# State-space tables for all rows at once on VectorE, each part's injection one part earlier, and half of the modulation rows in the attention-free branch's last product

## The chip, the cores and the metric

The kernel runs on one core of one Trainium2 chip. The metric is the device time of one execution in microseconds (us). Three executions of the kernel before took 1556.84, 1557.27 and 1558.54 us; their median, 1557.27 us, is the time to compare with. The core has five engines with one in-order queue each: PE (TensorE, matmuls), DVE (VectorE), ACT (ScalarE), POOL (GpSimd) and SP, which here only issues DMAs; ACT issues some DMAs too.

## The reference

One decoder block on 1024 rows of width 1024. A conditioning vector gives twelve modulation rows of 512 values (six of 1024). A state-space branch and an attention branch read the same projection; a gated feed-forward follows.

```python
cond = silu(c)
sh1, sc1, g1, sh2, sc2, g2 = split(cond @ w_ada + b_ada, 6)     # 12 pieces of 512 columns, n = 0..11
h = rmsnorm(x, norm1_g) * (1 + sc1) + sh1
u, q, k, v, gate_a, gate_b = split(h @ w_in)
# state-space branch: 32 groups of 16 channels, 64 complex states each
lam_bar = exp(lam * dt);  b_bar = (lam_bar - 1) / lam * b
states  = scan(a * x + bu),  bu = u @ b_bar                       # over the 1024 rows
y = gelu(real(states @ c) + d_skip * u)
y = y * sigmoid(y @ w_glu + b_glu)                                # GLU
y_a = y @ w_a
y_b = stick_breaking_attention(q, k, v) @ w_b
x = x + g1 * ((sigmoid(gate_a) * y_a + sigmoid(gate_b) * y_b) @ w_o)
# modulation by sh2, sc2, then a SwiGLU feed-forward, times g2, and a last rmsnorm
```

## The kernel before

**Stages.** The block runs as a row of stages, and PE works through nearly all of them: the projection to u (0 to 101 us), then a middle stage (101 to 316 us) in which PE makes v (`v_proj`, 16 tiles of 24 matmuls, 128x256) and the first gates (`gate(0, m)`, 16 tiles of 24 matmuls, 128x512) while the state-space branch is worked out in pieces beside it; the GLU (316 to 339); q and k of the first pair of heads (`qk_proj`, 339 to 361); `branch_a`, the product with w_a times the gate (361 to 404); then attention, the output projection and the feed-forward. Each fp32 product is made as three products of split operands (a high part and a low part), and the splits (`wh`, `wl`, `wgh`, `wgl`, line 417 on ACT and line 420 on DVE) are made just ahead of the use of a weight.

**The state-space branch in four parts.** Part m is 8 of the 32 groups. The 1024 rows are cut into 128 chunks of 8: within a chunk the sum is a small dense product, and between chunks a scan over 128 values carries the state. A part has these steps:

- `tables(m)`: POOL makes the rotation tables `tc`, `tn` (128 partitions x 4 x 128) by seven doublings of a complex product (`cmul`, six instructions each, lines 71 to 76), and then the injection `er`, `ei` (two copies, lines 223 and 224, and three doublings). PE transposes the injection (line 236, 8 matmuls), and ACT copies it to `inj`. DVE makes `o` (lines 249 to 251, six instructions of 128x576), PE multiplies it by `bst` (line 259, 16 matmuls), ACT copies that to `rt`, DVE adds the skip (lines 264, 266), and eight DMAs lay it out as `tz`.
- `run(m)`: eight DMAs bring u; PE injects it (line 288, 32 matmuls); DVE turns the result by the tables (lines 296 to 301, six instructions of 128x512) and scans it (line 304, eight instructions). The turn back takes four products: two on DVE (lines 310, 311) and two on POOL (lines 314, 315). DVE combines them into `h` (lines 318 and 319, two instructions each), PE makes y from u and h (lines 326 and 327, 16 matmuls each), ACT copies it, eight DMAs store it to `yD`.

`glu` then loads all of y (`raw`), ACT makes the gelu, and ACT and DVE split it into `yp` (lines 904, 905), which the GLU's matmuls read.

**The modulation rows.** Pieces 0 to 3 of `w_ada` are used at the start. Pieces 4 to 11 go through `ada_rest`: SP loads two of eight slices at a time (`aw`, 512 KB, two buffers), DVE multiplies each slice by its eight values of cond and adds it to `acc` (line 868 first, then seven times line 870), and SP stores `acc` to `aD`. Before, all eight pieces are called in the middle stage, two behind each `run(m)`. The rows are read back after attention.

**What sets the order.** A scheduler at build time gives each engine's queue its order from the program's dependencies and costs; the order in the source is only where it starts. At run time each queue is worked strictly in order and stops where its next instruction's operands are not ready. The pool `scr` has six buffers of 128x576 for temporaries; `acc` has two. `branch_a` has 16 tiles; for each, SP loads a gate tile `sg` (three buffers), ACT takes its sigmoid, PE makes 12 matmuls into `ga` (four PSUM buffers), DVE multiplies (line 951) into `gst`, and ACT's queue stores that to `nD`.

Of the kernel before, what the change touches and what calls it, by code (L numbers as in the profile page):

```python
# [28 lines left out]
class S5:  # L29
# [169 lines left out]
    def tables(self, m):  # L199

        nc, pool, work = self.nc, self.pool, self.work
        v, gp = nc.vector, nc.gpsimd
        r0 = slice(4 * m, 4 * m + 4)
        g0 = slice(8 * m, 8 * m + 8)

        tc_ = work.tile([128, 4, 128], F32, name="tc", bufs=2)
        tn = work.tile([128, 4, 128], F32, name="tn", bufs=2)
        p1 = work.tile([128, 4, 64], F32, name="p1", bufs=1)
        p2 = work.tile([128, 4, 64], F32, name="p2", bufs=1)
        gp.memset(tc_[:, :, 0:1], 1.0)  # L210
        gp.memset(tn[:, :, 0:1], 0.0)
        for k in range(7):
            n = 1 << k
            sh = [128, 4, n]
            self.cmul(gp, tc_[:, :, n:2 * n], tn[:, :, n:2 * n], tc_[:, :, 0:n], tn[:, :, 0:n],
                      self.wr[:, r0, k + 1:k + 2].broadcast_to(sh), self.wi[:, r0, k + 1:k + 2].broadcast_to(sh),
                      p1[:, :, :n], p2[:, :, :n])

        er = self.scr([4, 8, 16])
        ei = self.scr([4, 8, 16])  # L220
        p1 = p1.rearrange("p r (j i) -> p r j i", i=16)
        p2 = p2.rearrange("p r (j i) -> p r j i", i=16)
        gp.tensor_copy(er[:, :, 7], self.bbr[:, r0])
        gp.tensor_copy(ei[:, :, 7], self.bbi[:, r0])
        for n in (1, 2, 4):
            src, dst = slice(8 - n, 8), slice(8 - 2 * n, 8 - n)
            sh = [128, 4, n, 16]
            self.cmul(gp, er[:, :, dst], ei[:, :, dst], er[:, :, src], ei[:, :, src],
                      self.lpr[:, r0, n:n + 1].unsqueeze(3).broadcast_to(sh),
                      self.lpi[:, r0, n:n + 1].unsqueeze(3).broadcast_to(sh),  # L230
                      p1[:, :, :n], p2[:, :, :n])
        inj = work.tile([128, 2, 4, 128], F32, name="inj")
        for k, e in ((0, er), (1, ei)):
# [3 lines left out]
            nc.scalar.copy(inj[:, k].rearrange("p r q -> p (r q)"), ps)  # L237

# [33 lines left out]
        return tc_, tn, inj, o, tz  # L272

    def run(self, m, tabs, u_src, y_dst):
# [3 lines left out]
        tc_, tn, inj, o, tz = tabs  # L278
        u = work.tile([128, 8, 128], F32, name="u")
# [29 lines left out]
        gp = nc.gpsimd.tensor_tensor  # L309
        tt(m1[:, :, a], gr[:, :, a], tc_[:, :, a], ALU.mult)  # L310
        tt(m2[:, :, a], gi[:, :, a], tn[:, :, a], ALU.mult)
        m3 = self.scr([4, 128])
        m4 = self.scr([4, 128])
        gp(m3[:, :, a], gi[:, :, a], tc_[:, :, a], ALU.mult)
        self.last = gp(m4[:, :, a], gr[:, :, a], tn[:, :, a], ALU.mult)
        for g in range(2):
            q = slice(64 * g, 64 * g + 64)
            tt(h[0:64, :, g, b], m1[q, :, a], m2[q, :, a], ALU.subtract)
            tt(h[64:128, :, g, b], m3[q, :, a], m4[q, :, a], ALU.add)
# [71 lines left out]
class Block:  # L391
# [112 lines left out]
    def start(self, const, up, s5p):  # L504
# [5 lines left out]
        self.cond32 = up.tile([P, KT, 32], F32, name="cond32")  # L510
        nc.vector.tensor_scalar(self.cond32, self.cond.unsqueeze(2).broadcast_to([P, KT, 32]), 1.0 / 32.0, None, ALU.mult)
        self.hT = [[self.PA.tile([P, 2, 512], F32R, name="pa") for _ in range(KT)], []]
        with self.pool("s0", 1, side="right") as sp, self.pool("s0a", 1, side="right") as ap, self.pool("s5t", 1, side="right") as st, \
                self.pool("s0p", 1, PSUM) as pp, self.pool("s0t", TPB, PSUM) as tp, self.pool("s0m", 5 - TPB, PSUM) as mp:
            x = [None] * KT
# [31 lines left out]
            def ada(g):  # L547
# [15 lines left out]
                for a in (2 * g, 2 * g + 1):  # L563
                    ws.append(self.u_weight(a, ring=None if a < 3 else (up, "u3h", "u3l", self.wring[0][3], "ws", 2)))
# [292 lines left out]
    def ada_rest(self, n, ap, first):  # L857
# [78 lines left out]
    def branch_a(self, y2p, tp, gp):  # L936
# [352 lines left out]
    def run(self):  # L1289
        tc, nc, i = self.tc, self.nc, self.i  # L1290
        with ExitStack() as es:
# [18 lines left out]
            with ExitStack() as s1:  # L1310
# [6 lines left out]
                with self.pool("us", 1, side="right") as up, self.pool("s5", 1, side="right") as pool:  # L1317
                    self.start(const, up, pool)
                    with self.pool("s5w", 1, side="right") as work, self.pool("vs", 2, side="right") as vp, \
# [3 lines left out]
                        s5.begin(work, psum)  # L1323
                        for m in range(4):
# [7 lines left out]
                with ExitStack() as s3:  # L1332
                    with self.pool("ta", 2, side="right") as tp, \
# [10 lines left out]
                        self.branch_a(y2p, tp, gp)  # L1344
# [73 lines left out]
```

## Time and profile before

| | |
|---|---|
| runs shown | 1556.84, 1557.27, 1558.54 us (median 1557.27) |
| profiled execution | 1554.78 us, of which the span of instructions is 1553.1 us |
| granted TensorE clock, mean | 0.965 |
| PE busy | 1416.7 us (91% of the span) |
| PE weight loads | 1115.9 us (72%) |
| DVE busy | 1060.9 us (68%) |
| ACT busy | 612.8 us (39%) |
| POOL busy | 801.9 us (52%) |
| moved by DMA | 210.46 MB, mean 136 GB/s |

Busy time counts matmuls whose ends are modelled, so 91% on PE is not 91% of PE's peak. In the views below a line "A <- B: t, n" says that engine A stood idle t us in n places until B was done. A window row gives its start and end, its length, then for each engine busy time and, in brackets, the number of instructions that started in it; then the granted clock (1.00 is full), the busy share of the DMA engines (it can pass 1 in a short window) and the GB/s moved. Line numbers are those of the kernel before; in the changed kernel the same statements stand five to nine lines lower.

### The profile page before, as it was taken

What the parts mean: (1) busy time and instruction counts of PE and PEld (TensorE: products, weight loads), DVE (VectorE), ACT (ScalarE), POOL (GpSimd) and SP (SyncE); (2) the same over time, 40 slices, a digit from 0 to 9 for tenths busy, and PEclk for the clock granted to TensorE, in tenths of its full rate; (3) what the DMA queues carried; (4) which work ended last, traced back from release to release, by engine and by line L of the source; (5) the groups of instructions that cost most, each with busy time, mean ns of one, the idle gap of its engine ahead of it and who ended that gap; (6) DMA issues with size and microseconds to landing.
All of it is one profiled execution on the core that took longest, in us unless ns stands there. A gap on an engine that the chain in (4) does not pass through costs nothing.

```text
span 1553.1 us, 18339 instructions
## 1 busy us (share of the span) xinstructions
PE 1416.7 (91%) x6578; PEld 1115.9 (72%) x6578; DVE 1060.9 (68%) x1319; ACT 612.8 (39%) x792; POOL 801.9 (52%) x633
## 2 busy tenths in 40 slices
PE   4898889799999999988799889999999998999995
PEld 2687767678765556556688668888888887788874
DVE  5548777542467676775724797666666767999998
ACT  5431211352466656564314643223332323443323
POOL 2488694010346565642420015555555469698795
PEclk9899899899999999999899999999999999999998
DMA  8456775645424233336343413333333137454412
GB/s 274 171 141 182 180 192 170 178 123 158 144 89 129 82 97 115 109 102 208 118 163 114 138 47 118 108 105 110 107 108 112 63 123 296 149 162 148 122 57 109
DMA packets 180451, 210.46 MB, mean 136 GB/s; under 512 B 28612, under 2 KB 121896, under 8 KB 180360
## 3 DMA queue, kind: packets, MB, share of 16 engines
q1 hardware_dynamic: 169288, 201.29, 41.2%
q10 hardware_dynamic: 11072, 8.00, 1.8%
q8 instruction: 52, 0.85, 0.2%
q14 instruction: 39, 0.32, 0.1%
HBM read 159.18 MB, written 48.89 MB: 134 GB/s over the span
## 4 chain that ended last, share of the span: by engine, by line
PE 30%; DVE 10%; POOL 5%; issue 5%; DMA 1%; ACT 1%; DVEq 0%; POOLq 0%; ACTq 0%
PE tq L1136 12%; PE wo L1136 9%; PE wo L1017 5%; PE gu L1136 3%; POOL pb L1196 1%; POOL pa L1189 1%; DVE f L1220 1%; POOL wb L1218 1%; DMA pa<-in_w_ffn_down_dram 1%; DVE x L1241 1%; DVE pb L1241 1%; POOL x L1196 1%; DVE wl L1216 1%; DVE f L1216 1%; DVE ft L436 1%
## 5 line engine op out<-in xcount | busy, mean ns | idle before, releaser
L436 POOL TENSOR_TENSOR ws<-wb 128x1024 f32<-128x1024 f32 x26 | 64.2, 2471 | 193.4 <-DVE f L1043 90.0
L801 POOL TENSOR_TENSOR wa<-wa,wb 128x1024 f32<-128x1024 f32 (+2 forms) x32 | 81.2, 2538 | 72.8 <-DVE wa L797 49.4
L420 POOL TENSOR_TENSOR wl<-ws,wh 128x1024 fp32r<-128x1024 f32 x14 | 39.0, 2787 | 118.3 <-ACT wh L417 108.1
L769 DVE TENSOR_TENSOR wl<-ws,wh 128x1024 fp32r<-128x1024 f32 (+1 forms) x40 | 52.7, 1317 | 67.4 <-POOL wh L768 67.3
L436 POOL TENSOR_TENSOR wgs<-wb 128x1024 f32<-128x1024 f32 x14 | 35.6, 2542 | 72.7 <-DVE wgl L439 31.2
L802 ACT ACTIVATE wa<-wa 128x1024 f32<-128x1024 f32 (+1 forms) x40 | 38.9, 971 | 82.4 <-POOL wa L801 81.3
L1189 POOL TENSOR_TENSOR pa<-pa,row 128x1024 f32<-128x1024 f32 x22 | 66.1, 3026 | 1.3 <-DMA pa<-in_w_ffn_down_dram 1.3
L870 DVE SCALAR_TENSOR_TENSOR acc<-aw,cond,acc 128x512 f32<-128x512 f32 x56 | 54.2, 970 | 17.6 <-DMA aw<-in_w_ada_dram 17.0
L768 POOL TENSOR_SCALAR wh<-ws 128x1024 fp32r<-128x1024 f32 (+1 forms) x40 | 38.4, 959 | 50.1 <-DVE ws L767 48.8
L1127 POOL TENSOR_TENSOR f<-f,f 128x512 f32<-128x512 f32 x30 | 49.0, 1660 | 26.1 <-DVE f L1117 17.6
L767 DVE SCALAR_TENSOR_TENSOR ws<-wa,ws 128x1024 f32<-128x1024 f32 (+1 forms) x40 | 53.4, 1334 | 13.1 <-ACT ws L766 12.8
L699 PE MATMUL mm<-wa,V 128*64 128x512 f32 (+3 forms) x192 | 40.7, 517 | 20.7 <-ACT wa L802 20.7
L417 ACT CAST wh<-ws 128x1024 fp32r<-128x1024 f32 x28 | 29.2, 1047 | 56.9 <-PE wo L1017 31.6
L764 ACT ACTIVATE ws<-wa 128x1024 f32<-128x1024 f32 (+1 forms) x40 | 38.7, 969 | 29.2 <-DVE wa L761 28.8
L1218 POOL TENSOR_TENSOR wb<-pa 128x512 f32<-128x512 f32 x23 | 40.1, 1753 | 15.7 <-DVE wxl L1216 5.5
L797 DVE TENSOR_TENSOR wa<-wa,acc 128x512 f32<-128x512 f32 (+1 forms) x80 | 46.6, 616 | 1.1 <-PE acc L699 1.1
L1116 ACT ACTIVATE f<-f 128x1024 f32<-128x1024 f32 x22 | 23.3, 1061 | 57.0 <-DVE f L1156 29.5
L699 PE MATMUL z<-q,k 64*128 64x512 f32 (+3 forms) x192 | 41.8, 526 | 2.2 <-DVE gst L951 2.2
L1127 POOL TENSOR_TENSOR f<-f 128x512 f32<-128x512 f32 x20 | 42.2, 2127 | 0.0
L1235 PE MATMUL wo<-f,f 128*128 128x512 f32 x132 | 40.7, 389 | 0.0
L766 ACT ACTIVATE ws<-ws 128x1024 f32<-128x1024 f32 (+1 forms) x40 | 38.9, 974 | 1.1
L765 ACT ACTIVATE ws<-ws 128x1024 f32<-128x1024 f32 (+1 forms) x40 | 38.8, 971 | 1.1
(810 smaller groups left out, 4797.5 us busy)
## 6 DMA issues: line engine op xcount, KB each, us to landing
aw<-in_w_ada_dram SPq DMA_DIRECT2D x32, 512.0 KB
wb<-cD SPq DMA_DIRECT2D x32, 512.0 KB
hD<-f SPq DMA_DIRECT2D x30, 512.0 KB
ws<-in_w_in_dram SPq DMA_DIRECT2D x23, 512.0 KB
wb<-in_w_ffn_gate_dram SPq DMA_DIRECT2D x44, 256.0 KB
wb<-in_w_ffn_up_dram SPq DMA_DIRECT2D x44, 256.0 KB
pa<-in_w_ffn_down_dram SPq DMA_DIRECT2D x22, 512.0 KB
wb<-hD SPq DMA_DIRECT2D x40, 256.0 KB
```

The lines of the kernel that those rows point to most:

```text
L436: (add or nc.gpsimd).tensor_tensor(st, a, b, op)
L699: return self.tc.keep_in_program_order(self.nc.tensor.matmul(*args, **kw))
L767: nc.vector.scalar_tensor_tensor(st, a, 0.0, st, ALU.max, ALU.add)
L769: nc.vector.tensor_tensor(lt, st, ht.bitcast(F32), ALU.subtract)
L797: nc.vector.tensor_tensor(a[:, x, 0:f], a[:, x, 0:f], r[:, x, 0:f], ALU.subtract)
L801: nc.gpsimd.tensor_tensor(a[:, :, o], a[:, :, o], behind[:, :, old], ALU.subtract)
L870: nc.vector.scalar_tensor_tensor(acc, w[:, j], cj, acc, ALU.mult, ALU.add)
L1017: nc.tensor.matmul(ps, lhsT=mg[t // 4][k][:, a, P * (t % 4):P * (t % 4) + P], rhs=ws[k // 2][b][:, k % 2], start=(j == 0), stop=(j == 23))
L1127: nc.gpsimd.tensor_tensor(o, a, b, op)
L1136: self.nc.tensor.matmul(ps, lhsT=w[x][:, q, k], rhs=self.B[i](y, k), start=(j == 0), stop=(j == 11))
L1189: nc.gpsimd.tensor_tensor(w, w, g2, ALU.mult)
L1218: last_sum = nc.gpsimd.tensor_tensor(st[:, R], u, W[p][b[0]][:, 512 * b[1]:512 * b[1] + 512], SIGN_B[i])
```

## The change

Three things are changed together.

1. **Tables.** `phases()` makes `tc` and `tn` for all 16 rows (128 x 16 x 128) at once, on DVE, before the first part; POOL makes none. `inject(m)` makes the injection on DVE (its two copies on ACT), in buffers of its own (`e`, two of 128x512). The products of lines 314 and 315 go to DVE. `scr` has four buffers instead of six. `tc`, `tn` and the small temporaries take space that the first stage uses, and `cond32`, `u3h` and `u3l` move into a pool that is released at the end of that stage.
2. **Order of the parts.** `inject(m + 1)` is called inside `run(m)`, ahead of y's matmuls, and `outputs(m + 1)` (the part of `tables` that makes `o`, `rt` and `tz`) behind them. u has two buffers.
3. **Modulation rows.** `aw` now holds one slice (256 KB) and `acc` has one buffer. The middle stage makes pieces 4 to 7, one for each part. Pieces 8 to 11 are made in `branch_a`, with six `aw` buffers, and their loads wait for the last sigmoid of the GLU.

```diff
-        t = self.work.tile([128, 576], F32, name="scr", bufs=6)[:, 0:n]
+        t = self.work.tile([128, 576], F32, name="scr", bufs=4)[:, 0:n]
-    def tables(self, m):
+    def phases(self):
+        self.tc_ = tc_ = work.tile([128, 16, 128], F32, name="tc", bufs=1)
+        self.tn = tn = work.tile([128, 16, 128], F32, name="tn", bufs=1)
+        p1, p2 = (work.tile([128, 16, 64], F32, name=k) for k in ("y", "h"))
         for k in range(7):
             n = 1 << k
-            sh = [128, 4, n]
-            self.cmul(gp, tc_[:, :, n:2 * n], tn[:, :, n:2 * n], tc_[:, :, 0:n], tn[:, :, 0:n],
+            sh = [128, 16, n]
+            self.cmul(v, tc_[:, :, n:2 * n], tn[:, :, n:2 * n], tc_[:, :, 0:n], tn[:, :, 0:n],
...
+    def inject(self, m):
+        er, ei = (work.tile([128, 4, 8, 16], F32, name="e", bufs=2) for _ in range(2))
+        nc.scalar.copy(er[:, :, 7], self.bbr[:, r0])
+        nc.scalar.copy(ei[:, :, 7], self.bbi[:, r0])
         for n in (1, 2, 4):
-            self.cmul(gp, er[:, :, dst], ei[:, :, dst], er[:, :, src], ei[:, :, src],
+            self.cmul(v, er[:, :, dst], ei[:, :, dst], er[:, :, src], ei[:, :, src],
...
-        gp(m3[:, :, a], gi[:, :, a], tc_[:, :, a], ALU.mult)
-        self.last = gp(m4[:, :, a], gr[:, :, a], tn[:, :, a], ALU.mult)
-        for g in range(2):
-            q = slice(64 * g, 64 * g + 64)
-            tt(h[0:64, :, g, b], m1[q, :, a], m2[q, :, a], ALU.subtract)
-            tt(h[64:128, :, g, b], m3[q, :, a], m4[q, :, a], ALU.add)
+        for rows, x, z, op in ((slice(0, 64), gr, gi, ALU.subtract), (slice(64, 128), gi, gr, ALU.add)):
+            tt(m1[:, :, a], x[:, :, a], tc_[:, :, a], ALU.mult)
+            tt(m2[:, :, a], z[:, :, a], tn[:, :, a], ALU.mult)
+            for g in range(2):
+                q = slice(64 * g, 64 * g + 64)
+                tt(h[rows, :, g, b], m1[q, :, a], m2[q, :, a], op)
+        if more:
+            self.inject(m + 1)
         y = work.tile([128, 8, 128], F32, name="y")
...
+        if more:
+            self.outputs(m + 1)
...
-AK, ARB = 2, 2
+AK, ARB = 1, 2
...
-        acc = ap.tile([P, 512], F32, name="acc", bufs=2)
+        acc = ap.tile([P, 512], F32, name="acc")
-            w = ap.tile([P, AK, 512], F32, name="aw", bufs=ARB)
+            w = ap.tile([P, AK, 512], F32, name="aw", bufs=bufs)
...
+            for n in ((8, 9), (10,), (11,), ())[c]:
+                self.ada_rest(n, ap, self.sig, 6)
...
-                            s5.run(m, s5.tables(m), self.uD[P * m:P * m + P], self.yD[P * m:P * m + P])
-                            for n in (4 + 2 * m, 5 + 2 * m):
-                                self.ada_rest(n, ap, self.upin)
+                            s5.run(m, self.uD[P * m:P * m + P], self.yD[P * m:P * m + P], m < 3)
+                            self.ada_rest(4 + m, ap, self.upin)
```

**Where the next part's injection stands.** Before, it is on POOL. These rows of POOL's queue are those between part 0 and part 1: the end of part 1's rotation tables, the two products of part 0's turn back (which need both of part 0's scans on DVE), and behind them the start of part 2's tables and of part 1's injection.

```order
L75 TENSOR_TENSOR tc<-tc,p_1166 128x4x64
L76 TENSOR_TENSOR tn<-tn,p_1167 128x4x64
L314 TENSOR_TENSOR scr<-scr,tc 128x4x127
L315 TENSOR_TENSOR scr<-scr,tn 128x4x127
L210 MEMSET tc 128x4
L223 COPY scr<-bbr 128x4x16
L73 TENSOR_TENSOR tc<-tc,wr 128x4
L72 TENSOR_TENSOR p_1167<-scr,lpi 128x4x16
```

After, POOL's queue has none of these. On DVE the injection of part 2 (the rows with `e`) stands between part 0's turn (`s5s`), scans (`rho`) and turn back, with slices of a modulation row (`acc`) between.

```order
L304 TENSOR_TENSOR scr<-scr 128x512
L72 TENSOR_TENSOR p_1284<-e,lpi 128x4x16
L73 TENSOR_TENSOR e<-e,lpr 128x4x16
L875 SCALAR_TENSOR_TENSOR acc<-aw,cond,acc 128x512
L305 TENSOR_TENSOR scr<-s5s_1062,tc 128x512
L306 TENSOR_TENSOR scr<-s5s_1053,tn 128x512
L310 SCALAR_TENSOR_TENSOR scr<-rho,scr 128x128 x4
L71 TENSOR_TENSOR p_1283<-e,lpi 128x4x16
L74 TENSOR_TENSOR e<-e,lpr 128x4x16
L655 COPY vst<-mx 128x256
L875 SCALAR_TENSOR_TENSOR acc<-aw,cond,acc 128x512
L307 TENSOR_TENSOR scr<-scr 128x512
```

What moved: an injection that had to wait on POOL for the scans of the part ahead is now in DVE's own queue, ahead of those scans.

**DVE in `branch_a`.** Before, its queue holds the splits of w_a, two copies of k, and the 16 products with the gate.

```order
L420 TENSOR_TENSOR wl<-ws,wh 128x1024
L680 COPY k<-qx 128x512
L680 COPY k<-mm 128x512
L420 TENSOR_TENSOR wl<-ws,wh 128x1024
L951 TENSOR_TENSOR gst<-ga,sg 128x512 x4
L420 TENSOR_TENSOR wgl<-wgs,wgh 128x1024
L951 TENSOR_TENSOR gst<-ga,sg 128x512 x12
```

After, the slices of pieces 8 to 11 stand between them; this is the stretch from the last copy of k to the second split of w_a behind it.

```order
L685 COPY k<-mm 128x512
L875 SCALAR_TENSOR_TENSOR acc<-aw,cond,acc 128x512
L425 TENSOR_TENSOR wl<-ws,wh 128x1024
L875 SCALAR_TENSOR_TENSOR acc<-aw,cond,acc 128x512
L958 TENSOR_TENSOR gst<-ga,sg 128x512
L875 SCALAR_TENSOR_TENSOR acc<-aw,cond,acc 128x512 x2
L958 TENSOR_TENSOR gst<-ga,sg 128x512
L875 SCALAR_TENSOR_TENSOR acc<-aw,cond,acc 128x512
L958 TENSOR_TENSOR gst<-ga,sg 128x512 x2
L873 TENSOR_SCALAR acc<-aw,cond 128x512
L425 TENSOR_TENSOR wgl<-wgs,wgh 128x1024
```

What moved: each product with the gate now stands behind slices that wait for their own loads, and SP's queue holds those 32 loads between the loads of the gate tiles.

More of the change, by code (lines that the diff above doesn't have):

```diff
@@ L237, in tables, with outputs @@
             nc.scalar.copy(inj[:, k].rearrange("p r q -> p (r q)"), ps)
+        self.inj = inj
+    def outputs(self, m):
+        nc, work = self.nc, self.work
+        v, gp = nc.vector, nc.gpsimd
+        g0 = slice(8 * m, 8 * m + 8)
         o = work.tile([128, 8, 9, 16], F32, name="o")
@@ L271, in tables, with run @@
             eng.dma_start(out=tz[16 * j:16 * j + 16, :, 16 * j:128], in_=rt[:, :, 0:128 - 16 * j])
-        return tc_, tn, inj, o, tz
-    def run(self, m, tabs, u_src, y_dst):
+        self.o, self.tz = o, tz
+    def run(self, m, u_src, y_dst, more):
         nc, work = self.nc, self.work
         v = nc.vector
-        tc_, tn, inj, o, tz = tabs
-        u = work.tile([128, 8, 128], F32, name="u")
+        inj, o, tz = self.inj, self.o, self.tz
+        tc_, tn = (t[:, 4 * m:4 * m + 4] for t in (self.tc_, self.tn))
+        u = work.tile([128, 8, 128], F32, name="u", bufs=2)
         for j in range(8):
@@ L934, in halves, with branch_a @@
         return [[t[:, :, k, 512 * h:512 * h + 512] for k in range(4)] for h in range(2)]
-    def branch_a(self, y2p, tp, gp):
+    def branch_a(self, y2p, tp, gp, ap):
         nc, i = self.nc, self.i
@@ L1343, in run @@
                         self.mm = Turns((ga, "ga"))
-                        self.branch_a(y2p, tp, gp)
+                        with self.pool("ar2", 1, side="right") as ap:
+                            self.branch_a(y2p, tp, gp, ap)
                     self.exp_ln()
```

40 lines of the change are left out of this document (14 added, 26 removed).

## The prediction

> **What bounds the kernel now.** I read the stages by windows first, because the chain of waits of the page reaches back from the end only to about the middle of the span and says nothing of the part that is changed.
>
> ```profile
> 101.00:316.00 215.00, 183.10 (x1122) 159.95 (x1121) 145.90 (x198) 44.04 (x63) 134.88 (x265) 0.91 0.68 185
> 339.00:361.00 22.00, 22.00 (x98) 18.22 (x98) 6.00 (x6) 6.02 (x10) 4.30 (x6) 1.00 0.44 131
> 361.00:404.00 43.00, 43.00 (x191) 35.59 (x191) 12.73 (x17) 11.58 (x16) 4.79 (x2) 1.00 0.64 205
> ```
>
> The columns are start, end, length, then busy time and starts on PE, PE's weight loads, DVE, ACT and POOL, then the granted clock, the DMA share and GB/s. In the middle stage PE is idle 215 - 183.1 = 31.9 us and its clock is not full; in the two stages behind it PE has no gap. So what can be gained lies in 101 to 316. What ends PE's gaps there, by its waits from 101 to 320:
>
> ```profile
> PE s5a L236 <- POOL scr L75: 19.8, 4, 7.2
> PE s5a L327 <- DVE h L319: 6.6, 2, 6.3
> PE s5a L327 <- DVE h L318: 1.6, 1, 1.6
> ```
>
> Of 31.9 us, 19.8 are the transposes of the injection waiting for POOL's last doubling, once in each part, and 8.2 are y waiting for `h`. What a gap costs beyond itself, in windows of 5 us:
>
> ```profile
> 105.00:110.00 5.00, 5.00 (x44) 5.00 (x43) 0.42 (x1) 0.37 (x1) 5.00 (x20) 1.00 1.08 245
> 125.00:130.00 5.00, 5.00 (x50) 4.48 (x50) 2.61 (x4) 1.15 (x2) 5.00 (x20) 0.85 0.71 256
> 160.00:165.00 5.00, 0.00 (x0) 0.00 (x0) 5.00 (x6) 0.00 (x0) 5.00 (x6) 0.57 0.72 188
> 165.00:170.00 5.00, 4.40 (x21) 4.40 (x22) 2.19 (x2) 0.84 (x2) 5.00 (x17) 0.50 0.76 167
> 290.00:295.00 5.00, 3.30 (x13) 2.41 (x12) 1.60 (x2) 2.99 (x4) 0.00 (x0) 0.84 0.94 252
> 295.00:300.00 5.00, 5.00 (x19) 3.94 (x19) 1.98 (x2) 0.96 (x2) 0.00 (x0) 0.78 0.80 250
> 300.00:305.00 5.00, 5.00 (x24) 4.14 (x23) 0.34 (x1) 4.58 (x5) 0.00 (x0) 1.00 0.84 250
> ```
>
> PE is empty from 160 to 165, and in the next 5 us, behind that gap, the clock is 0.50.
>
> From these rows I take what PE needs at full clock. A v matmul takes 5/44 = 0.114 us, one of 128x512 43.00/191 = 0.225 us, and one of the state-space pieces 5/50 = 0.100 us (that window is mostly theirs, at a clock of 0.85, so it is an upper value). The stage has 384 of the first, 384 of the second, and 4 x (8 + 16 + 32 + 32) = 352 of the third: 43.8 + 86.4 + 35.2 = 165.4 us. From 101 that ends at 266.4, and the GLU begins at 316. So 50 us is all that this stage can give: 31.9 of gaps, the rest half clock.
>
> **Why POOL is late.** Its waits and its instructions, 93 to 320:
>
> ```profile
> POOL scr L314 <- DVE scr L304: 33.5, 3, 24.1
> L314 POOL TENSOR_TENSOR scr<-scr,tc 128x508 f32<-128x508 f32 x4 | 10.1, 2518 | 45.8 <-DVE scr L304 33.5 <-PE mm L625 12.3
> L71 POOL TENSOR_TENSOR p<-tn,wi 128x4 f32<-128x4 f32 x4 | 7.2, 1808 | 0.0
> L75 POOL TENSOR_TENSOR tc<-tc,p 128x256 f32<-128x256 f32 x4 | 4.2, 1055 | 0.0
> ```
>
> POOL's queue has the injection of the next part behind line 314, which waits for this part's scans: parts cannot overlap. When it is free, it is slow: 1055 ns for 256 elements, and an instruction of 4 elements takes 1808 ns on average when DVE works beside it.
>
> **The change part by part.** DVE's prices, 93 to 320 (busy us, mean ns of one), with line 870 also by its shortest, median and longest, and two splits in a row:
>
> ```profile
> L870 DVE SCALAR_TENSOR_TENSOR acc<-aw,cond,acc x56: 729/752/6721, 114.5 to 274.2; 128x512 f32<-128x512 f32 x56
> L870 DVE SCALAR_TENSOR_TENSOR acc<-aw,cond,acc 128x512 f32<-128x512 f32 x56 | 54.2, 970 | 17.6 <-DMA aw<-in_w_ada_dram 17.0
> L304 DVE TENSOR_TENSOR_SCAN scr<-rho,scr 128x128 f32<-128x128 f32 x32 | 11.4, 414 | 0.0
> L319 DVE TENSOR_TENSOR h<-scr 64x508 f32<-64x508 f32 x8 | 5.5, 683 | 0.2
> L301 DVE TENSOR_TENSOR scr<-scr 128x512 f32<-128x512 f32 x4 | 2.7, 670 | 0.0
> L264 DVE TENSOR_TENSOR dd<-ident,dT 16x128 f32<-16x128 f32 x4 | 1.1, 272 | 0.0
> L661 DVE COPY gst<-mm 128x512 f32<-128x512 f32 x4 | 2.7, 682 | 1.9 <-PE mm L625 1.9
> L650 DVE COPY vst<-mm 128x256 f32<-128x256 f32 x4 | 1.7, 419 | 10.1 <-PE mm L646 10.1
> 294.62 1.22 DVE L420 TENSOR_TENSOR wgl<-wgs,wgh 128x1024 fp32r<-128x1024 f32 x1 [0.98 <-ACT wgh L417]
> 295.76 1.22 DVE L420 TENSOR_TENSOR wl<-ws,wh 128x1024 fp32r<-128x1024 f32 x1
> ```
>
> Behind the split at 294.62 the next starts 1.14 us later, so 0.08 us of a duration is overlapped. That makes 0.60 us for 512 elements, 1.14 for 1024, hence about 0.05 us fixed and 0.00107 us an element. DVE's own work from 101 to the last `h`:
>
> - `phases`: 42 products over 6 x 16 x 127 = 12192 elements: 13.0 + 42 x 0.05 = 15.1 us.
> - `inject`: 4 x 18 products, 2688 elements a part: 4 x (2.9 + 0.9) = 15.2 us.
> - `outputs`: 24 x 0.67 for 128x576, and eight small ones at 0.2: 17.7 us.
> - `run`: a part has 10 products at 0.60, 8 scans at 0.33 (414 ns less the overlap) and 4 halves of `h` at 0.60, 11.0 us; four parts 44.2. The products of lines 314 and 315 are in it: 1.2 us a part on DVE that POOL did in 2.5 and more.
> - slices: 32 where there were 64, at 0.66 (the median of line 870 is 752 ns, its mean of 970 has those that run beside POOL): 21.1 us.
> - copies and splits up to there: eight `vst` at 0.34, five `gst` at 0.60, seven splits at 1.14: 13.7 us.
>
> Together 127 us. It cannot start before the u projection's last matmul, about 101, since `tc` now takes the space of `u3l`:
>
> ```profile
> L584 PE MATMUL mm<-pb,u3l x8: 389/389/389, 96.8 to 101.1; 128*128 128x512 f32 x8
> L210 POOL MEMSET tc<- x4: 99/103/105, 94.0 to 197.5; 128x4 f32 x4
> ```
>
> POOL began at 94.0. That costs little, since from 105 to 110 DVE was busy 0.42 us. With no wait at all DVE would be done at 228, ahead of PE. So POOL's work is bought for 30 us of DVE, and 21 us of slices leave it: the stage's DVE load hardly moves, but nothing of a part stands behind another part any more. The 19.8 us of PE's first row go. The 8.2 us of waits for `h` shrink with the lines 318 and 870 that ran beside POOL.
>
> **What is late next: the slices' loads.** DVE waits, 93 to 320, and SP's:
>
> ```profile
> DVE acc L870 <- DMA aw<-in_w_ada_dram: 17.0, 9, 3.8
> DVE acc L868 <- DMA aw<-in_w_ada_dram: 9.3, 4, 5.6
> SPq L864 <- DVE acc L870: 25.4, 15, 6.2
> L864 SPq DMA_DIRECT2D aw<-in_w_ada_dram x32: 368/389/628, 109.1 to 269.2; - x32
> L868 DVE TENSOR_SCALAR acc<-aw,cond x8: 468/569/1504, 113.4 to 258.8; 128x512 f32<-128x512 f32 x8
> ```
>
> There were 32 loads of 512 KB in two buffers; there are now 32 of 256 KB in two buffers, so only half as much is ahead. From the first issue (109.1) to the first use (113.4) is 4.3 us. Before, DVE waited 26.3 us for 32 loads. What it waits now is bounded by nothing below (all loads hidden by the work between the slices) and by a whole round trip for every pair above: 16 x 4.3 = 69 us. I take the 26.3 of the nearest row: as many loads, at a like rate. Also each piece's first slice now waits for the store of the one `acc`, three times at most, inside this bound. On SP, u, `tz` and the y stores stand behind these waits; SP waited 25.4 us for slices before, and I leave that as it is.
>
> The Trainium skill ("DMA: Bandwidth & Descriptors", Anatomy of one DMA) puts about 2.0 us fixed on every DMA whatever its size and then 436 GB/s. By it a 256 KB load takes an estimated 2.6 us, not half of the larger load's time, and 16 pairs would give 42 us where I take 26.3; my last y would then come 15 us later. No run so far shows a 256 KB load of `aw`.
>
> So DVE's last `h` is at 228 + 26 = 254, y's last matmuls 2 us behind it, 256. PE by itself would be there at:
>
> ```profile
> L326 PE MATMUL s5a<-u,tz x64: 272/275/421, 141.1 to 290.3; 128*128 128x128 f32 x64
> L327 PE MATMUL s5a<-h,o x64: 271/275/581, 153.3 to 290.5; 128*128 128x128 f32 x64
> 304.66 1.23 DVE L905 TENSOR_TENSOR yp<-y,yp 128x1024 fp32r<-128x1024 f32 x1 [7.67 <-DMA raw<-yD]
> 319.29 1.23 DVE L905 TENSOR_TENSOR yp<-y,yp 128x1024 fp32r<-128x1024 f32 x1 [2.70 <-ACT yp L904]
> ```
>
> From the last y matmul (290.5) to the GLU (316) there are 25.5 us, with the same gate tiles as cover behind y's store, the gelu and the splits; 12 matmuls fewer ran from 290 to 300 than at full clock, some 2.5 us. So PE's floor for the last y is 266.4 - 23 = 243, and DVE with its loads sets it, at 256. PE and DVE also wait for each other at the injections and `h` of the parts; PE has 13 us of room, and I add 2 us: 258. The GLU moves from 316 by 290.5 - 258 = 32.5 us. Its last operand (`yp`, 319.29) follows the last y at the same distance, so the GLU's own wait stays.
>
> **What comes back in `branch_a`.** 32 slices are 21 us of DVE in a stage where it has room (6.0 and 12.7 busy of 22 and 43), and 8.4 MB of loads. What it moved before: 22 x 131 + 43 x 205 = 11.7 MB in 65 us; now 20.1 MB, 309 GB/s. The profile's row of 40 slices, and DVE's longest wait from 361 to 407:
>
> ```profile
> GB/s 274 171 141 182 180 192 170 178 123 158 144 89 129 82 97 115 109 102 208 118 163 114 138 47 118 108 105 110 107 108 112 63 123 296 149 162 148 122 57 109
> DVE gst L951 <- DMA nD<-gst: 20.6, 8, 4.3
> ```
>
> The most over 39 us is 296. At 296 the stage takes 68 us, at 274 it takes 73: 3 or 8 us come back if everything has to land inside it. DVE already waits there for stores of `gst`. Some loads belong to later stages, which speaks for less; none at all is the lower bound. I take 4 us. Where this cover is gone, PE waits for a `ga` buffer. Attention and what follows have the same order on all engines but for single swaps, and I cost them at nothing.
>
> **Sum.** Against the profiled execution: 1554.8 - 32.5 + 4 = 1526.3. It stands 2.5 us below the median of the runs, so the median should be 1557.3 - 28.5 = 1528.8; I say 1529.
>
> **The rivals.** *DVE's loads take twice what I give them* (52 us): last y at 284, gain 6.5 - 4, 1555 with 4 given back, 1551 with nothing. For it: two buffers of half the size, slices that stand two to four in a row on DVE. Against it: most slices have 1 to 4 us of other work between them. *The other side:* slower than before, by the same mechanism alone, if the loads take more than 32.5 + 26 - 4 = 54 us, 1.7 us each; at the bound of 69 it ends at 1557 + 14 = 1571. *PE is the bound:* loads hidden, last y at 245, gain 45 with nothing back: 1512; for it, DVE's 15 us of room; against, 26.3 us of measured waits with more work between. *`branch_a` gives back its worst:* DVE's products with the gate stand behind slices, stores to `nD` take longer, 8 to 12 us back: 1533 to 1537. *The change does nothing on time:* `h` takes the place of the injection as the wait, at the same rhythm (line 327 goes from 153.3 to 290.5, 45.7 us a part); DVE's 127 us over four parts is 32 a part, so this needs 13 us of waits in each.
>
> **How the numbers follow.** The likeliest case, DVE with its loads as the bound, 1519 to 1540, 0.58; PE bound, below 1519, 0.14; loads at up to twice, 1540 to 1554, 0.17; no change 0.04; slower 0.07. What runs of this kernel can tell from no change is 0.2%, about 3 us. Faster is then 0.89, same 0.04, slower 0.07. `branch_a`'s worst lies inside the forecast's range. The range that leaves out 0.2 is 1512 to 1550: below it the best third of the PE-bound case (0.05), above it no change, slower, and the worst of the loads (0.15); its upper end is loads at 1.8 times the row I took.
>
> **What would show it.** After: no wait of PE for POOL in this stage; POOL's busy time lower by over 100 us; DVE's slices at 0.75 us each; waits for `aw` near 26 us; the GLU's first matmul near 284; in `branch_a` PE with gaps of a few us and 300 GB/s. It is wrong if PE's idle time from 101 to the GLU is above 30 us again, if waits for `aw` pass 50 us, or if `branch_a` takes over 50 us.

## The result, and the profile after

The changed kernel takes 1531.77 us (median of 4 runs, 1530.32 to 1535.52) against 1557.9 us for the kernel before on the same chip: a ratio of 0.9848, with a 95% interval of 0.9829 to 0.9866. It is 26 us faster; 1529 was forecast. Run again later with other versions, it came to 0.9845 (0.9819 to 0.9871). The profiled execution took 1532.77 us, with a span of 1530.4; the one of before took 1554.78.

The stages of the changed kernel, in the same columns as before (the third and fourth rows are `branch_a` and the time from its last matmul to attention's first):

```profile
101.00:280.00 179.00, 172.92 (x1127) 151.37 (x1126) 138.41 (x297) 44.66 (x71) 4.07 (x8) 0.98 0.63 168
303.00:325.00 22.00, 22.00 (x99) 18.22 (x98) 11.41 (x14) 6.10 (x10) 4.35 (x6) 1.00 0.86 268
325.00:374.00 49.00, 44.70 (x194) 35.71 (x192) 28.98 (x40) 10.69 (x15) 5.43 (x3) 1.00 0.90 298
374.00:383.00 9.00, 0.21 (x2) 0.21 (x4) 2.73 (x4) 1.61 (x3) 3.35 (x3) 0.64 0.65 209
```

The middle stage is 179 us long instead of 215. PE's idle time in it fell from 31.9 to 6.1 us, its clock rose from 0.91 to 0.98, and POOL, busy for 134.9 us before, is busy for 4.1. Behind it, `branch_a` took 43 us and now takes 49, and then PE stands still for 9 us. Its waits from 95 to 420:

```profile
PE z L704 <- DVE gst L958: 8.9, 1, 8.9
PE mm L651 <- DVE wl L425: 4.7, 1, 4.7
PE ga L630 <- DVE gst L958: 4.2, 3, 1.9
```

The waits for POOL are gone. The longest wait now is that of attention's first matmul (`z`) for the last product with the gate, which was 2.2 us before:

```profile
PE z L699 <- DVE gst L951: 2.2, 1, 2.2
```

The matmuls that mark the steps, y's second factor, the GLU and attention (lines 327, 625 and 699 before; in the state-space branch lines moved by other amounts than the five to nine given above):

```profile
L330 PE MATMUL s5a<-h,o x64: 271/275/275, 172.5 to 255.5; 128*128 128x128 f32 x64
L630 PE MATMUL ga<-yp,wh x64: 387/389/496, 280.0 to 302.9; 128*128 128x512 f32 x64
L704 PE MATMUL z<-q,k x192: 272/589/694, 382.8 to 657.8; 64*128 64x512 f32 x96, 64*128 64x128 f32 x32, 64*128 64x256 f32 x32, 64*128 64x384 f32 x32
```

Set against the kernel before (290.5, 316.3, 406.9), the last y comes 35.0 us earlier, the GLU 36.3 us earlier, and attention 24.1. So 36.3 us were gained in the middle stage and 12.2 given back up to attention; the spans differ by 22.7.

All versions by these marks, in us of one profiled execution each, with the ratio of times; the experiments below have the labels of this table. The changed kernel and its repeat (`after_again`) differ by 0.3 to 0.4 us in the marks. The versions were timed in four groups, each beside the kernel before, whose median there was 1557.9 us (changed), 1554.7 (tables_only, mods_only, light, gst4), 1555.3 (six_two, inj_late, inj_pool, acc2) and 1554.2 (the last four rows), so versions of different groups are best compared by the ratio.

| version | last y | GLU starts | attention starts | median time | ratio to before, 95% interval |
|---|---|---|---|---|---|
| before | 290.5 | 316.3 | 406.9 | 1557.9 | |
| changed | 255.5 | 280.0 | 382.8 | 1531.8 | 0.9848 (0.9829 to 0.9866) |
| tables_only | 261.9 | 317.1 | 409.9 | 1557.6 | 1.0026 (1.0010 to 1.0042) |
| mods_only | 282.1 | 306.8 | 410.2 | 1556.0 | 1.0001 (0.9984 to 1.0017) |
| six_two | 257.9 | 287.5 | 380.3 | 1530.0 | 0.9843 (0.9817 to 0.9869) |
| inj_late | 266.9 | 289.1 | 392.5 | 1544.6 | 0.9938 (0.9918 to 0.9958) |
| inj_pool | 244.8 | 284.4 | 384.7 | 1533.5 | 0.9869 (0.9836 to 0.9902) |
| light | 257.1 | 281.5 | 370.9 | 1517.8 | 0.9763 (0.9745 to 0.9782) |
| gst4 | 257.8 | 282.3 | 376.6 | 1528.6 | 0.9833 (0.9804 to 0.9863) |
| acc2 | 255.4 | 279.6 | 378.1 | 1527.1 | 0.9819 (0.9792 to 0.9846) |
| after_again | 255.2 | 279.6 | 383.1 | 1529.9 | 0.9845 (0.9819 to 0.9871) |
| gst4acc2 | 254.2 | 278.3 | 372.9 | 1529.3 | 0.9830 (0.9807 to 0.9853) |
| acc2_six | 259.7 | 289.2 | 384.2 | 1534.4 | 0.9867 (0.9845 to 0.9888) |
| acc2_six_pool | 254.2 | 284.6 | 385.0 | 1528.2 | 0.9829 (0.9805 to 0.9853) |

### The profile page after: what moved, and what is told of

It is laid out like the page before. It is cut to its first block, busy times and chain, and to the rows that moved or that the text cites. A ratio compares the mean times of both kernels' runs of the same rounds, so it can differ in the third digit from the quotient of the medians.

```text
span 1530.4 us, 18295 instructions
## 1 busy us (share of the span) xinstructions
PE 1409.0 (92%) x6578; PEld 1107.5 (72%) x6578; DVE 1072.2 (70%) x1443; ACT 614.0 (40%) x800; POOL 663.2 (43%) x369
## 4 chain that ended last, share of the span: by engine, by line
PE 45%; DVE 19%; DMA 12%; issue 10%; POOL 9%; ACT 4%; SPq 1%; ACTq 0%; POOLq 0%; DVEq 0%
PE tq L1143 12%; PE wo L1143 9%; PE wo L1024 5%; PE gu L1143 3%; PE mm L589 3%; PE mm L704 2%; POOL wa L806 2%; PE ga L630 2%; PE mx L704 2%; POOL wh L773 1%; PE mx L630 1%; POOL pb L1203 1%; DMA aw<-in_w_ada_dram 1%; DVE wa L802 1%; DVE acc L875 1%
## 5 line engine op out<-in xcount | busy, mean ns | idle before, releaser
L425 POOL TENSOR_TENSOR wl<-ws,wh 128x1024 fp32r<-128x1024 f32 x14 | 38.9, 2780 | 136.8 <-ACT wh L422 136.3
L875 DVE SCALAR_TENSOR_TENSOR acc<-aw,cond,acc 128x512 f32<-128x512 f32 x56 | 43.8, 782 | 9.9 <-DMA aw<-in_w_ada_dram 9.4
L273 POOL MEMSET tz<- 128x1024 f32 x4 | 3.8, 953 | 92.8 <-PE s5a L329 84.9
L771 ACT ACTIVATE ws<-ws 128x1024 f32<-128x1024 f32 (+1 forms) x40 | 39.0, 974 | 1.1
```

Of the source, the lines that this page charges most:

```text
L875: nc.vector.scalar_tensor_tensor(acc, w[:, j], cj, acc, ALU.mult, ALU.add)
```

## The experiments

### Half of the change at a time

The tables without the move of the slices (`tables_only`):

```diff
-                            self.ada_rest(4 + m, ap, self.upin)
+                            for n in (4 + 2 * m, 5 + 2 * m):
+                                self.ada_rest(n, ap, self.upin)
...
-            for n in ((8, 9), (10,), (11,), ())[c]:
-                self.ada_rest(n, ap, self.sig, 6)
```

> The changed kernel with all eight modulation pieces made in the middle stage (two behind each part, loads of 256 KB) and none in branch_a. Theory A (the gain is that a part's injection no longer stands on POOL behind the scans of the part ahead): PE does not wait for POOL in the middle stage, DVE has 21 us more there, so the last y comes 5 to 20 us later than in the changed kernel (255.5), the GLU starts at 285 to 300 instead of 280; branch_a is as in the kernel before (43 us, attention starts about 2 us behind it), so 10 to 12 us come back there: 1525 to 1540 us. Theory B (the gain is the slices that leave the middle stage): the GLU starts near 316 as before and the time is 1550 to 1560 us.

It took 1557.6 us, 0.3% more than before on the same chip: nothing is left of the gain, and theory A's time was missed by 18 us. Both numbers are those of theory B. Yet theory A's first step held, as the last y shows, and PE's waits say where the rest went:

```profile
L330 PE MATMUL s5a<-h,o x64: 271/275/377, 173.5 to 261.9; 128*128 128x128 f32 x64
PE ga L630 <- ACT yp L909: 25.8, 2, 25.3
PE mm L630 <- ACT wh L422: 5.8, 1, 5.8
```

The last y is 28.6 us earlier than before (261.9 for 290.5), for 6.4 us of delay against the changed kernel. But from there to the GLU are 55.2 us, where the kernel before has 25.8. DVE's timeline and SP's in that stretch:

```profile
305.92 0.75 DVE L875 SCALAR_TENSOR_TENSOR acc<-aw,cond,acc 128x512 f32<-128x512 f32 x1 [2.17 <-DMA aw<-in_w_ada_dram]
306.98 0.75 DVE L875 SCALAR_TENSOR_TENSOR acc<-aw,cond,acc 128x512 f32<-128x512 f32 x1 [0.31 <-DMA aw<-in_w_ada_dram]
317.17 1.22 DVE L910 TENSOR_TENSOR yp<-y,yp 128x1024 fp32r<-128x1024 f32 x1 [9.44 <-ACT yp L909]
```

```profile
297.23 6.87 SPq L869 DMA_DIRECT2D aw<-in_w_ada_dram  x4
307.76 0.33 SPq L876 DMA_DIRECT2D aD<-acc  x1
309.86 10.60 SPq L921 DMA_DIRECT2D raw<-yD  x6
```

The slices that no longer fit between the parts form a tail behind the last `h`. SP issues the loads of y (`raw`) only at 309.9, behind the last slice's load and the last store of `acc`, 48 us after the last y matmul. The tables' 28.6 us are spent waiting for slices that nobody needs yet. This version keeps the loads of 256 KB and the one `acc`, and in that stretch DVE waits 3.8 and 2.2 us for stores of `acc` too. The tables alone with 512 KB loads and two `acc`, as before the change, were not run.

The move of the slices without the tables (`mods_only`: the kernel before, with `ada_rest` and `branch_a` as in the changed one):

```diff
-                            for n in (4 + 2 * m, 5 + 2 * m):
-                                self.ada_rest(n, ap, self.upin)
+                            self.ada_rest(4 + m, ap, self.upin)
...
+            for n in ((8, 9), (10,), (11,), ())[c]:
+                self.ada_rest(n, ap, self.sig, 6)
```

> The kernel before (tables on POOL, part by part) with pieces 8 to 11 of the modulation made in branch_a as in the changed kernel, loads of 256 KB and one acc. Theory A: PE waits for POOL's injection some 20 us as before, the GLU starts at 300 to 316, branch_a and its handover give back about 12 us as in the changed kernel: 1553 to 1570 us. Theory B: the GLU starts at 280 to 290 and the time is 1530 to 1540 us.

1556.0 us, no difference from before, as theory A had it. PE's waits:

```profile
PE s5a L236 <- POOL scr L75: 13.1, 4, 4.2
PE z L699 <- DVE gst L953: 9.1, 1, 9.1
PE s5a L327 <- DVE h L319: 4.4, 1, 4.4
```

PE still waits for POOL in all four parts. The GLU starts 9.5 us earlier than before (306.8), and `branch_a` with its handover takes it back: attention starts at 410.2, 3.3 us later. So theory B (the slices alone) fails too: it had the GLU at 280 to 290. Neither half gains anything alone; together they gain 26 us.

Whether the tail costs, or each slice in the stage, was tried with six pieces there, two behind each of the first three parts, and two in `branch_a` (`six_two`):

```diff
-                            self.ada_rest(4 + m, ap, self.upin)
+                            for n in ((4, 5), (6, 7), (8, 9), ())[m]:
+                                self.ada_rest(n, ap, self.upin)
...
-            for n in ((8, 9), (10,), (11,), ())[c]:
+            for n in ((10,), (11,), (), ())[c]:
```

> The changed kernel with pieces 4 to 9 in the middle stage (two behind each of the first three parts, none behind the last) and only 10 and 11 in branch_a. The tables alone gave a last y at 261.9 but a GLU at 317.1, because DVE worked through slices until 307.0 and the loads of y stood behind their loads on SP. Theory T (what costs is the tail of slices behind the last h, not the slices as such): without a tail the GLU starts at 283 to 292, branch_a gives back half of what it does in the changed kernel (6 of 12 us), and the time is 1524 to 1533 us. Theory L (each piece in the middle stage costs the same, (317.1 - 280.0) / 4 = 9 us): the GLU starts near 298 and the time is 1536 to 1546 us.

```profile
L330 PE MATMUL s5a<-h,o x64: 271/275/377, 172.4 to 257.9; 128*128 128x128 f32 x64
L630 PE MATMUL ga<-yp,wh x64: 389/389/498, 287.5 to 309.7; 128*128 128x512 f32 x64
```

The GLU starts at 287.5 and the time is 1530.0: theory T in both numbers. With 16 of the 32 moved slices back in the stage, the last y is late by 2.4 us only, and DVE's slices end at 260.7, where they ended at 307.7 with all eight pieces. That speaks for the tail as the cost; all eight pieces without a tail were not tried. What the later GLU loses, the lighter `branch_a` saves: from the GLU to attention are 92.8 us, so 2.2 come back there, where theory T had 6.

### What makes the parts overlap

The injection of the next part called behind the y stores instead of ahead of y's matmuls (`inj_late`):

```diff
-        if more:
-            self.inject(m + 1)
         y = work.tile([128, 8, 128], F32, name="y")
...
         if more:
+            self.inject(m + 1)
             self.outputs(m + 1)
```

> The changed kernel with the injection of the next part called behind the y stores instead of ahead of y's matmuls. If making it ahead is what takes PE's wait away, PE waits again for DVE's injection, 3 to 7 us in each of three parts, and the time rises by 8 to 20 us over the changed kernel (about 1531). If DVE's speed does it wherever the injection stands, the time is within 3 us of 1531.

1544.6 us, 13 us slower than the changed kernel: the injection ahead of time is worth about half of the gain. The time is that of the first answer; the wait that I named did not come. Of PE's waits, 95 to 300, the two longest and the one for the injection:

```profile
PE s5a L327 <- DMA tz<-rt: 6.0, 1, 6.0
PE s5a L328 <- DVE h L320: 3.7, 1, 3.7
...
PE s5a L264 <- ACT inj L235: 0.2, 1, 0.2
```

PE does not wait for the injection (0.2 us) but for what stands behind it: `tz` and `h`, with the last y at 266.9, 11.4 us later.

The injections on POOL, called where the changed kernel calls them (`inj_pool`):

```diff
-            self.cmul(v, er[:, :, dst], ei[:, :, dst], er[:, :, src], ei[:, :, src],
+            self.cmul(nc.gpsimd, er[:, :, dst], ei[:, :, dst], er[:, :, src], ei[:, :, src],
```

> The changed kernel with the 18 products of each injection on POOL instead of DVE, called at the same place; the rotation tables and all of the turn back stay on DVE. If POOL's queue order was the trouble (the injection behind products that waited for scans), POOL is free now and makes each injection a part ahead: no wait of PE for it, DVE has 15 us less, and the time is 1527 to 1533 us. If POOL's speed beside DVE was the trouble (1 to 5 us an instruction), PE waits 3 us and more in each part and DVE's instructions stretch: 1536 us or more.

1533.5 us, half a us above the first answer and not distinguishable from the changed kernel; the interval of its ratio (0.9836 to 0.9902) takes that one in. The last y came at 244.8, 10.7 us earlier: PE's queue has fewer instructions ahead of it (949 start from 101 to the last y, 1025 in the changed kernel). Yet the GLU came 4.4 us later. From the last y to the GLU PE is busy nearly all the time in both (39.6 of 39.6 us here, 23.7 of 24.5 there), so the GLU's start follows the time that PE loses on the way, and its idle time from 101 to the GLU rose from 6.1 to 11.5 us. Most of that is one instruction on POOL's timeline, for which PE waits:

```profile
126.32 1.60 POOL L74 TENSOR_TENSOR e<-e,lpr 128x256 f32<-128x256 f32 x1
127.88 7.97 POOL L75 TENSOR_TENSOR e<-e,p 128x256 f32<-128x256 f32 x1
135.81 0.73 POOL L76 TENSOR_TENSOR e<-e,p 128x256 f32<-128x256 f32 x1
```

```profile
PE s5a L234 <- POOL e L75: 11.5, 2, 10.9
```

The instruction behind it, of the same shape, took 0.73 us; this one took 7.97. So both halves of the question hold: with POOL's queue in order the other three injections cost PE 0.6 us, and POOL beside a busy DVE is slow by bursts.

### What comes back in `branch_a`

The price of the slices there, by leaving most of them out (`light`):

```diff
-        for k in range(0, KT, AK):
+        for k in range(0, KT if bufs == ARB else 1, AK):
```

> The changed kernel with only the first of eight slices of pieces 8 to 11 loaded and added (7 MB of loads and 28 DVE instructions of branch_a left out, so those modulation rows are not the reference's). If what comes back between the GLU and attention is the price of these slices, attention's first product starts 10 to 13 us earlier than in the changed kernel (382.8) and the time is 1517 to 1522 us: the ceiling of the change. If the stores with two buffers cost it by themselves, it stays within 3 us of 1531.

1517.8 us, and attention starts at 370.9, 11.9 us earlier. From the GLU to attention are 89.4 us, as before the change (90.6), where the changed kernel has 102.8. So these slices cost 12 to 14 us, and this is about the ceiling: 37 us (a ratio of 0.9763) would be gained if they were free. DVE's work and the loads were left out together, so this does not say which of the two costs. What they do in the changed kernel, by DVE's waits from 303 to 384 and its last products with the gate:

```profile
DVE gst L958 <- DMA nD<-gst: 14.4, 7, 4.8
DVE acc L873 <- DMA aD<-acc: 7.0, 2, 6.1
...
DVE acc L873 <- DMA aw<-in_w_ada_dram: 3.4, 2, 1.8
DVE acc L875 <- DMA aw<-in_w_ada_dram: 3.2, 5, 0.8
```

```profile
375.88 0.69 DVE L958 TENSOR_TENSOR gst<-ga,sg 128x512 f32<-128x512 f32 x1 [1.22 <-DMA nD<-gst]
378.56 0.69 DVE L958 TENSOR_TENSOR gst<-ga,sg 128x512 f32<-128x512 f32 x1 [2.00 <-DMA nD<-gst]
382.04 0.69 DVE L958 TENSOR_TENSOR gst<-ga,sg 128x512 f32<-128x512 f32 x1 [2.79 <-DMA nD<-gst]
```

Four products are still to be made when PE starts its last matmul of `branch_a`, at 373.5. The last three, shown here, go one by one, each behind the store of the tile two before. The slices' own loads are waited for less (6.6 us for 32 loads, with six buffers). With them the DMA engines move 298 GB/s in that stage (211 in `light`, 205 before). Before, DVE waited even longer for these stores (20.6 us), but PE waited only 2.2 us for the last product: what is new is that DVE is behind when the stage ends.

Four buffers for these products (`gst4`):

```diff
-                    o = gp.tile([P, 512], F32, name="gst")
+                    o = ap.tile([P, 512], F32, name="go", bufs=4)
```

> The changed kernel with four instead of two buffers for branch_a's products with the gate. Theory G (DVE is late at the end of branch_a because each product waits for a store of two tiles before): DVE's waits for the stores (14.4 us in the changed kernel) go below 4, PE's wait at attention's first product (8.9 us) falls to 2 to 4 and its three waits inside branch_a go: 1521 to 1526 us. Rival (the DMA engines are full, 298 GB/s in that stage): the waits turn into waits for gate tiles or slices, and the time stays at 1528 to 1534 us.

1528.6 us, the rival's time, and its interval (0.9804 to 0.9863) does not separate it from the changed kernel. The waits for stores went, and as the rival has it others came:

```profile
DVE go L958 <- ACT sg L954: 11.8, 6, 3.8
DVE acc L873 <- DMA aD<-acc: 8.4, 2, 6.5
DVE upto L695 <- POOL tri L693: 6.4, 1, 6.4
```

DVE now waits for the sigmoid of gate tiles, which arrive late. Attention starts 6.2 us earlier (376.6), but its last score matmul comes only 1.5 us earlier (656.3 for 657.8). Part of the reason stands in the trace: POOL makes attention's constants (`tri`, `mask`) at 307.5 to 309.4 us in the changed kernel, but from 381.2 here, behind a store of these products, and DVE's first use of the scores (`wa`) comes only 1.1 us earlier. Here, and in the changed kernel:

```profile
382.97 0.29 DVE L695 CAST upto<-tri 128x128 fp32r<-128x128 f32 x1 [6.37 <-POOL tri L693]
383.45 0.96 DVE L766 TENSOR_TENSOR wa<-z,mask 128x768 f32<-128x768 f32 x1 [0.20 <-POOL mask L700]
```

```profile
384.54 0.96 DVE L766 TENSOR_TENSOR wa<-z,mask 128x768 f32<-128x768 f32 x1 [1.81 <-PE z L704]
```

Two buffers for `acc` (`acc2`):

```diff
-        acc = ap.tile([P, 512], F32, name="acc")
+        acc = ap.tile([P, 512], F32, name="acc", bufs=2)
```

> The changed kernel with two buffers for acc instead of one. DVE waited 7.0 us for stores of acc at the start of branch_a and in it. If that is on the path to attention's first product (382.8), it starts 3 to 7 us earlier and the time is 1525 to 1529 us; if the products with the gate are late for their own stores and loads, nothing moves: 1530 to 1533 us.

1527.1 us, attention at 378.1: 4.7 us earlier, which is the first answer. DVE no longer waits 6 us at the second piece for the store of the first. The interval (0.9792 to 0.9846) overlaps that of the changed kernel.

### Combinations

The changed kernel again, and three versions beside it: two `acc` buffers with six pieces in the middle stage; these two with the injections of parts 1 to 3 on POOL; two `acc` buffers with four product buffers (`after_again`, `acc2_six`, `acc2_six_pool`, `gst4acc2`). The edits are those above, but for one:

```diff
-            self.cmul(v, er[:, :, dst], ei[:, :, dst], er[:, :, src], ei[:, :, src],
+            self.cmul(nc.gpsimd if m else v, er[:, :, dst], ei[:, :, dst], er[:, :, src], ei[:, :, src],
```

> The changed kernel once more, in the same call as the three versions below, so that they can be compared on one chip: 1528 to 1534 us, ratio to before 0.982 to 0.987.

> The changed kernel with two acc buffers, and pieces 4 to 9 in the middle stage (two behind each of the first three parts), 10 and 11 in branch_a. If the GLU's later start (287.5 with six pieces) and the shorter stay in branch_a cancel and acc's stores are what is left, attention's first product starts at 374 to 378 and the time is 1523 to 1527 us; if the second acc gains only because branch_a is crowded, it is no better than with six pieces alone, 1528 to 1531 us.

> As the version with two acc buffers and six pieces in the middle stage, with the injections of parts 1 to 3 on POOL (part 0's on DVE). DVE has 11 us less: if DVE is what the last y waits for with six pieces (257.9), the last y comes at 245 to 250 and the time falls by 4 to 8 us more, 1517 to 1523. If POOL's products beside DVE stretch (one took 8 us when all injections were on POOL), PE waits for them and the time is 1525 us or more.

> The changed kernel with two acc buffers and four buffers for the products with the gate. If stores of acc and of the products add up as waits on DVE's queue, attention's first product starts at 372 to 376 and the time is 1522 to 1526 us; if full DMA engines (298 GB/s) are the floor of branch_a, it is within 2 us of two acc buffers alone (1527).

On one chip: the changed kernel 1529.9, two `acc` with six pieces in the stage 1534.4, the same with three injections on POOL 1528.2, two `acc` with four product buffers 1529.3. The first of the two with six pieces missed both of its answers: attention starts at 384.2, later than with either edit alone. The second has the time of its second answer, but not for that reason: PE waits for POOL's injection only 1.4 us. The last y came at 254.2 where 245 to 250 was expected, 5.5 us earlier than without POOL, so DVE's 11 us were at most in part what it waited for. With four product buffers the waits do add up: attention starts at 372.9, 10.2 us ahead of the changed kernel run with it, as expected. But the time is not that of the first answer (1522 to 1526). From the first to the last score matmul it takes 280.1 us where the changed kernel takes 275.2, with `tri` late here too (378.0), so that profile's span is only 4.8 us shorter, and the medians differ by 0.6 us. None is shown to beat the changed kernel, and 1527.1 for two `acc` buffers was measured once. The runs of the changed kernel spread over 5 us in one group and 9 in the other, more than these differences.

## Why the prediction was right, point by point

**The size, 1529 for 1531.8.** It is inside the range and near the middle, but two terms were mis-sized against each other: the stage gave 36.3 us where I wrote 32.5, and 12.2 came back where I wrote 4. That the sum came out within 3 us is partly luck.

**PE's wait for POOL goes, and half clock with it: right.** 19.8 us of waits became none; the clock went from 0.91 to 0.98. POOL's busy time fell by 138.7 us (801.9 to 663.2 over the span); over 100 was forecast.

**DVE's work at its undisturbed price: right.** I counted 127 us up to the last `h`; DVE was busy 129.4 from 101 to 246. The slices took what I gave them, at a mean of 744 ns instead of 970, and the widest table products 1.2 us:

```profile
L875 DVE SCALAR_TENSOR_TENSOR acc<-aw,cond,acc 128x512 f32<-128x512 f32 x28 | 20.8, 744 | 6.3 <-DMA aw<-in_w_ada_dram 6.2
L75 DVE TENSOR_TENSOR tc<-tc,y 128x1024 f32<-128x1024 f32 x1 | 1.2, 1206 | 0.0
```

**Waits for slices in the middle stage, 26.3 us: mis-sized, 6.2.** The first of these two rows shows it (the 6.2 at its end); in the repeat it was 8.2. Smaller loads with work between them were nearly hidden, and the bound by round trips, 69, was far off. The Trainium skill's fixed time for a DMA ("DMA: Bandwidth & Descriptors", Anatomy of one DMA), which I had turned into 42 us of waits, does not decide here. That section of the Trainium skill gives its figures as a fit for DMAs issued by GpSimd, and not for every DMA as I wrote; these loads are issued by SP. First issue and first use of `aw` in the changed kernel:

```profile
L869 SPq DMA_DIRECT2D aw<-in_w_ada_dram x64: 327/333/2993, 109.0 to 359.1; - x64
...
L873 DVE TENSOR_SCALAR acc<-aw,cond x8: 468/483/486, 112.8 to 357.8; 128x512 f32<-128x512 f32 x8
```

The first 256 KB load was used 3.8 us after its issue, and DVE had other work until then, so this does not show how long the load took. What the waits show is that most of such times lay under other work.

**The last y at 258: right (255.5), and not for the reason given.** DVE's last `h` began at 245.7, not at 254, so DVE did not set it:

```profile
L320 DVE TENSOR_TENSOR h<-scr x16: 668/683/685, 161.1 to 245.7; 64x508 f32<-64x508 f32 x16
```

PE did, 12 us above the floor of 243 that I gave it: it is busy with matmuls of a gate until 252.1, without a gap from the last `h` on, and they stand ahead of y in its queue. So my likeliest case, DVE with its loads as the bound, is not what happened. It was nearer to the rival in which PE is the bound, to which I gave 0.14, with more lost on PE and in `branch_a` than its 1512 us allow. That 255.5 agrees with 258 is luck. Of the GLU's 13.6 us above its own floor of 266.4, 6.1 are gaps and some 4 the clock (0.02 of 179); the rest is not accounted for. One gap is a wait that I had not named: in the window before v's next tile PE has two matmuls in 5 us, while DVE's timeline has the last doubling of the wide tables ahead of the split of v's weight:

```profile
135.00:140.00 5.00, 0.30 (x2) 0.22 (x2) 5.00 (x8) 0.00 (x0) 0.00 (x0) 0.76 0.39 131
140.00:145.00 5.00, 5.00 (x26) 5.00 (x27) 5.00 (x8) 0.37 (x1) 0.11 (x1) 0.55 0.65 167
```

```profile
136.04 1.21 DVE L74 TENSOR_TENSOR tn<-tn,wr 128x1024 f32<-128x1024 f32 x1
...
138.52 1.21 DVE L425 TENSOR_TENSOR wl<-ws,wh 128x1024 fp32r<-128x1024 f32 x1
139.66 1.21 DVE L75 TENSOR_TENSOR tc<-tc,y 128x1024 f32<-128x1024 f32 x1
140.79 1.21 DVE L425 TENSOR_TENSOR wl<-ws,wh 128x1024 fp32r<-128x1024 f32 x1
```

That is the 4.7 us wait of v's matmul for `wl`, with half clock behind it.

**What comes back, 4 us: mis-sized, 12.2.** I worked out DMA traffic (309 GB/s; 298 measured) and took from it how much longer the stage would be. The step left out was the end: I wrote that PE waits for a `ga` buffer where the cover is gone, and it does, 4.2 us; but attention's first matmul waits for the last product, 8.9 us for 2.2 before, since DVE may be some products behind at the end while PE, with four `ga` buffers, has felt little of it. I had the row on which it hangs, 20.6 us of DVE's waits for stores of `gst`, and did not carry it to the end of the stage. Up to its last matmul `branch_a` took 49 us, just under the 50 that I had named as a sign of being wrong; with the 9 us at its end it is 58.

**The halves.** The forecast costed them as a sum; the runs showed that they need each other. I had said that the slices leaving the stage only keep DVE's load level. In fact they also free the way from y to the GLU, which is worth 31 us once the tables are done early (55.2 us in `tables_only`, 24.5 in the changed kernel), and 1 us before (25.8, and 24.7 in `mods_only`). I had left SP's waits as they were, and SP's queue is where the loads of y stood.

## What to carry to other kernels

When a chain is made shorter, ask what stands in the same queues behind its last link: here 28.6 us won at the last y vanished until the work that nobody waited for was taken out of SP's and DVE's queues ahead of the next stage. Work moved into a stage whose engine has room is still paid for at the stage's end, if that engine may lag there by a few buffers and the next stage waits for the last of them: read the first wait of the stage behind, not the busy share. A step that ends earlier is not yet a gain: y came 10.7 us earlier with the injections on POOL, and the GLU later. And run each half of a change alone before crediting either.

## What the runs showed of the hardware

Beside a busy DVE, single POOL instructions stretch by bursts: 128x256 products took 0.73 us and 7.97 us next to each other, with DVE busy without a gap around them (124.8 to 136.8 us). The mean of 1808 ns for 128x4 before is one instruction of 5.19 us and three of 0.7. With POOL nearly out of the way (4 us busy), DVE's slices fell from a mean of 970 to 744 ns; with the injections on POOL it was 814. A DVE product of 128x1024 with one operand broadcast along its inner dimension (line 74, by `wr`) cost the same as one without (line 75): 1.21 us each in the timeline above.
